# An output projection of eight K pairs as two products of 1024 columns, with the second half's keys rotated earlier, in a one-core encoder block

## The chip, the core and the metric

The kernel runs on one core of one Trainium2 chip. The core's engines work side by side, each with its own queue of instructions that it takes in order: TensorE (PE in the profile, with its weight loads as PEld), VectorE (DVE), ScalarE (ACT), GpSimd (POOL) and SyncE (SP), which here only issues transfers; 16 DMA engines carry data between HBM, in which inputs and weights lie, and the on-chip memory SBUF. TensorE writes into PSUM, a small memory of accumulators that VectorE and ScalarE read. A result passes from one engine to another by semaphores: an instruction that waits holds up everything behind it on its own engine.

The metric is the time of one execution on the device, in microseconds (us). Three executions of the kernel before took 1145.72, 1146.16 and 1146.77 us.

## The reference

One layer of an encoder over 256 tokens of width 2048, all in float32. Two groups of attention heads work side by side on the normalised input, and one matrix joins them:

```python
h = rms_norm(x, g_mix)
c_q, c_kv, k_rope, dq, dk, dv = jnp.split(h @ w_in, split_pts, axis=-1)
# latent attention: 8 heads with values of 128 -> out_mla (256 x 1024)
# differential attention: 4 heads, keys of 128, values of 256, rope on dq and dk
p1 = softmax(q1 @ k1.T * scale); p2 = softmax(q2 @ k2.T * scale)
o_diff = rms_norm((p1 - lam * p2) @ v, g_diff_sub, eps=1e-5) * (1 - lambda_init)
x = x + concatenate([out_mla, out_diff]) @ w_out          # 2048 x 2048
# cross attention: 4 heads of 128 into 256 tokens of mem
xq = rms_norm(x, g_xattn) @ w_xq
xk, xv = rms_norm(mem, g_mem) @ w_xk, rms_norm(mem, g_mem) @ w_xv
x = x + softmax(xq @ xk.T * scale) @ xv @ w_xo
# feed-forward with 5632 hidden columns
hf = rms_norm(x, g_ffn)
x = x + (silu(hf @ w_gate) * (hf @ w_up)) @ w_down
return rms_norm(x, g_final)
```

## The kernel before

**Matmuls.** Every float32 operand is split into a high part (`_h`), rounded to TensorE's float32r format, and a low part (`_l`), the remainder; a product is three matmuls, high by high, high by low and low by high (`mm`, L97 to L99). The split of weights costs ScalarE a cast (L105, `wh`) and VectorE a subtraction (L106, `wl`) for every 1024 columns of a 1 MB weight transfer (`wraw`, three buffers; `wh` and `wl` have four buffers each). The 256 tokens are two tiles of 128 (`tt` 0 and 1), the residual stream `x_res` (`xres0`, `xres1` in the profile) lies on chip as two tiles of 128 x 2048. Activations that go into a product lie transposed, four K blocks of 128 in a tile (`x0T`, `mixT`, `diffT`, `x1T`, `mT` ...).

**Two ways to multiply.** `project` makes 512 output columns from a list of weight pieces, with one accumulator for each token tile. `wide_project`, which before serves the feed-forward part alone, makes 1024 columns (two accumulators for each token tile) and goes over pairs of K blocks. A plain pair (`P`) is 2 x 2 x 2 products, 24 matmuls. A summed pair (`W`) takes a form of the product of two 2 x 2 block matrices with seven block products in place of eight, 21 matmuls. It needs sums of the activations' blocks (`summed_pair`: tiles `sums`, `forms`), sums of the weights' blocks (`tsum`), and four further accumulators (`q1`, `q5`, `q6`, `q7`) that are added at its end (`leave`), before the plain accumulators are (`join`). `_pairs` lays weights out in HBM for it, in the order `PLAIN` or `SUMS` of blocks.

**Stages.** The input projection and the latent attention come first and leave `mixT`, 8 K blocks. Differential attention comes in two halves of two heads each: `diff_project` and `diff_rope` make rotated queries and keys (`dT`), `values` the values (`val`), `diff_attend` scores (`psc`), softmax (`nm`, `e`, `rs`), the difference of two softmaxes (`e`), its transposes (`ppt`, `pT`), the product with the values (`pod`), the norm of each head (`ssd`, `rd`, on ScalarE, VectorE and GpSimd), the normalised head (`on`) and its transposes (`pdt`, `diffT`). The text order of the halves: queries, keys, values of the first half; queries of the second; attention of the first; keys and values of the second; attention of the second.

The output projection then comes in three pieces in columns of 512: `mixT` (8 K blocks), `diff0` (4), and, behind the keys of the memory (`mT` from a transfer with a gain, `w_xk`, `xkT`), `diff1` (4) inside `residual_T`. That function adds each column to `x_res`, transposes it with the gain of the next norm (`gT`, `x1T`) and sums its squares (`junk`). Cross attention and the feed-forward part follow.

**What sets the order.** The text names operations and dependences. A scheduler with a cost model of its own orders each engine's instructions when the kernel is built, and it interleaves stages: matmuls of a later stage stand between those of an earlier one where their operands and buffers allow it. The order on each engine is then fixed. Weight transfers keep the order of the text (`keep_in_program_order`), all on SP's queue. PSUM has eight banks: four accumulators (`acc_tile`) and four for everything else (`ps_tile`); `wide_project` swaps the two groups at its end.

Of the kernel before, what the change touches and what calls it, by code (L numbers as in the profile page):

```python
# [40 lines left out]
G_ORDER, U_ORDER = (0, 1, 2, 3, 4, 5, 6, 7), (0, 2, 1, 4, 3, 6, 5, 7)  # L41

# [36 lines left out]
def encoder_block(ctx: ExitStack, tc: tile.TileContext, a, out):  # L79
# [118 lines left out]
    def meansq(src, dst, cols, n):  # L198

        junk = sb.tile([P, 512], BF16, name="junk", tag="junk", bufs=1)  # L200
        nc.scalar.activation(junk[:, :cols], src, AF.Square, scale=n ** -0.5, accum_out=dst)

# [327 lines left out]
    def diff_attend(dq, dk, dv):  # L530
        mT = act_tile(name="diffT")
        ps_ = []
        for hh in range(2):
# [9 lines left out]
            ps_.append(e1)  # L543
        for hh in range(2):
# [19 lines left out]
            split_into(mT[:, 2 * hh:2 * hh + 2, :], pt.rearrange("p (e t) -> p e t", e=2))  # L564
        return mT
# [42 lines left out]
    def residual_T(src_accs, gain, name, raws=None):  # L608

        pieces = []  # L610
        ssq = small.tile([P, NT, 4], F32, name=name + "ss", tag=name + "ss", bufs=1)
        for oc in range(4):
            accs = src_accs(oc)
            t = act_tile(name=name)
            if raws is not None:
                raws.append(act.tile([P, 4, S], F32, name=name + "_f", tag="act"))
            for tt in range(NT):
                xs = x_res[tt][:, oc * 512:(oc + 1) * 512]
                nc.vector.tensor_tensor(out=xs, in0=xs, in1=accs[tt], op=ALU.add)
                transposed(t, xs, tt, 4, gain[:, 4 * oc:4 * oc + 4], raws and raws[oc])  # L620
                meansq(xs, ssq[:, tt, oc:oc + 1], 512, D)
            pieces.append(t)
        s1 = small.tile([P, NT], F32, name=name + "s1", tag=name + "s1", bufs=1)
        nc.vector.reduce_sum(out=s1, in_=ssq, axis=AX.X)
        r = rstd_of(s1, EPS, name + "r")
        return (lambda kt: pieces[kt // 4][:, kt % 4, :]), r
# [21 lines left out]
    x2raw = []  # L648
    x2T, rstdf = residual_T(
        lambda oc: project(lambda kt: xoT[:, kt, :], [a["w_xo"][oc, 0]]), g_f, "x2T", x2raw)  # L650
    soft_pool.close()
    attention.close()
    wsum = ctx.enter_context(tc.tile_pool(name="wsum", bufs=1))
    nat_pool[:] = wsum, 5


    def pair_raw(src):
        raw = wp.tile([P, 2048], F32, name="wraw", tag="wraw", bufs=3)
        raw = raw.rearrange("p (b c) -> p b c", b=4)
        tc.keep_in_program_order(nc.sync.dma_start(out=raw, in_=src))  # L660
        return raw

    def w_tile(n=2, pool=None):

# [4 lines left out]
    def split_blocks(src, pool=None):  # L669
        w = w_tile(src.shape[1], pool)  # L670
        split_into(w, src)
        return w

    class Pair:


        def __init__(self, plain=None, forms=None):
            self.plain, self.forms = plain, forms
# [351 lines left out]
```

## Time and profile before

| what | value |
|---|---|
| three executions | 1145.72, 1146.16, 1146.77 us |
| profiled execution | 1146.36 us |
| its span, from the first to the last instruction | 1144.6 us |
| mean granted clock of TensorE | 0.998 |
| TensorE busy | 1135.1 us (99%) |
| VectorE busy | 955.9 us (84%) |
| ScalarE busy | 636.2 us (56%) |
| GpSimd busy | 57.6 us (5%) |
| moved by DMA | 222.13 MB, 194 GB/s in the mean |
| transfers of w_out | 16 of 1 MB |

Busy times are sums over an engine's instructions in one profiled execution. Matmuls are pipelined, and the ends that the profile gives them are modelled, so that their pace is read from one start to the next. A name in the profile has a line of the kernel in front of it and shows a group of operations with the same output and input tiles. The chain of waits follows the work back from the last instruction, at each step to what released it. The granted clock is the share of full speed that the chip allowed TensorE.

In the trace the scores of the first half of differential attention lie around 250 us, the products of its probabilities and of the second half up to 290 us, the keys of the memory, the last piece of the output projection and the query of the cross attention from there to some 400 us; the feed-forward part fills the rest.

### The profile page before, as it was taken

To read this page: it belongs to the slowest core of one execution; us is meant where nothing else is said; L and a number is where in the kernel's file an instruction comes from. 1 tells how busy PE (TensorE), PEld (TensorE's weight loads), DVE (VectorE), ACT (ScalarE), POOL (GpSimd) and SP (SyncE) were. 2 spreads that over 40 slices of the span, in tenths; PEclk is the share of its full clock that TensorE was granted. 3 is DMA by queue.
4 is the path that set the end of the run, shared out by engine and by line. 5 is a ranking of instruction groups with operands and counts; after the bars stand their busy time and mean duration, and the time that the engine had idled before them with its cause. 6 is when DMAs were issued, how large, how long until landed. Compare 5 with 4: busy or idle time off the path is not lost.

```text
span 1144.6 us, 14297 instructions
## 1 busy us (share of the span) xinstructions
PE 1135.1 (99%) x5405; PEld 950.7 (83%) x5405; DVE 955.9 (84%) x1281; ACT 636.2 (56%) x897; POOL 57.6 (5%) x75
## 2 busy tenths in 40 slices
PE   9999999999999999999999999999999999999997
PEld 7888888888888888888888888888888888888886
DVE  6688766686868667989899998998999898998975
ACT  6755454454566455656465564665554564664642
POOL 4920000000000000000000000000000000000000
PEclk9999999999999999999999999999999999999999
DMA  9655335444854444455565556556555555565543
GB/s 358 221 194 187 143 113 182 154 178 155 318 194 179 148 166 169 180 192 208 197 212 194 182 213 221 184 187 218 184 190 215 201 204 191 195 242 202 195 171 129
DMA packets 34197, 222.13 MB, mean 194 GB/s; under 512 B 4176, under 2 KB 4944, under 8 KB 9808
## 3 DMA queue, kind: packets, MB, share of 16 engines
q1 hardware_dynamic: 32688, 216.73, 53.2%
q0 software_dynamic: 864, 3.15, 0.7%
q10 hardware_dynamic: 576, 1.34, 0.3%
q8 instruction: 42, 0.69, 0.2%
q14 instruction: 27, 0.22, 0.1%
HBM read 219.11 MB, written 2.10 MB: 193 GB/s over the span
## 4 chain that ended last, share of the span: by engine, by line
PE 98%; issue 0%; DMA 0%; DVE 0%; ACT 0%; DVEq 0%; POOLq 0%; POOL 0%; ACTq 0%
PE acc L97 27%; PE acc L98 26%; PE acc L99 26%; PE q L97 3%; PE q L99 3%; PE q L98 3%; PE pt L333 2%; PE ppt L480 1%; PE psc L99 1%; PE psc L98 1%; PE psc L97 1%; PE acckv L97 0%; PE acckv L98 0%; PE acckv L99 0%; PE pt L863 0%
## 5 line engine op out<-in xcount | busy, mean ns | idle before, releaser
L105 ACT CAST wh<-wraw 128x1024 fp32r<-128x1024 f32 (+2 forms) x400 | 392.5, 997 | 352.2 <-PE acc L99 305.5
L106 DVE TENSOR_TENSOR wl<-wraw,wh 128x1024 fp32r<-128x1024 f32 (+2 forms) x400 | 458.2, 1159 | 122.9 <-ACT wh L105 120.8
L98 PE MATMUL acc<-wl,x2n_h 128*128 128x512 f32 x320 | 124.5, 390 | 0.0
L99 PE MATMUL acc<-wh,x2n_l 128*128 128x512 f32 x320 | 123.9, 389 | 0.0
L106 DVE TENSOR_TENSOR wl<-tsum,wh 128x1024 fp32r<-128x1024 f32 x86 | 104.7, 1220 | 12.2 <-ACT wh L105 12.2
L105 ACT CAST wh<-tsum 128x1024 fp32r<-128x1024 f32 x86 | 90.2, 1050 | 42.7 <-DVE tsum L730 14.4
L97 PE MATMUL acc<-wh,x2n_h 128*128 128x512 f32 x320 | 109.7, 390 | 0.0
L98 PE MATMUL acc<-wl,x0T_h 128*128 128x512 f32 x224 | 88.3, 395 | 0.0
L99 PE MATMUL acc<-wh,x0T_l 128*128 128x512 f32 x224 | 88.2, 395 | 0.0
L97 PE MATMUL acc<-wh,x0T_h 128*128 128x512 f32 x224 | 87.3, 395 | 0.8 <-ACT x0T_h L108 0.8
L98 PE MATMUL acc<-wl,hT_h 128*128 128x512 f32 x188 | 73.3, 392 | 0.0
L99 PE MATMUL acc<-wh,hT_l 128*128 128x512 f32 x188 | 72.4, 389 | 0.0
L99 PEld LDWEIGHTS acc<-wh,x2n_l 128*128 128x128 f32 x320 | 60.1, 188 | 12.4
L98 PEld LDWEIGHTS acc<-wl,x2n_h 128*128 128x128 f32 x320 | 60.1, 188 | 12.3
L97 PEld LDWEIGHTS acc<-wh,x2n_h 128*128 128x128 f32 x320 | 59.9, 188 | 12.3
L98 PE MATMUL q<-wl,forms_h 128*128 128x512 f32 x172 | 66.9, 389 | 0.0
L99 PE MATMUL q<-wh,forms_l 128*128 128x512 f32 x172 | 66.7, 389 | 0.0
L97 PE MATMUL acc<-wh,hT_h 128*128 128x512 f32 x188 | 64.5, 391 | 0.0
L97 PE MATMUL q<-wh,forms_h 128*128 128x512 f32 x172 | 59.9, 389 | 0.0
L98 PE MATMUL acc<-wl,forms_h 128*128 128x512 f32 x149 | 57.8, 389 | 0.0
L99 PE MATMUL acc<-wh,forms_l 128*128 128x512 f32 x149 | 57.8, 389 | 0.0
L97 PE MATMUL acc<-wh,forms_h 128*128 128x512 f32 x149 | 57.0, 389 | 0.0
(382 smaller groups left out, 2258.0 us busy)
## 6 DMA issues: line engine op xcount, KB each, us to landing
wraw<-in_w_gate SPq DMA_DIRECT2D x44, 1024.0 KB, 4.8
wraw<-in_w_up SPq DMA_DIRECT2D x44, 1024.0 KB, 4.8
wraw<-in_w_dn SPq DMA_DIRECT2D x41, 1024.0 KB, 4.8
wraw<-in_w_in SPq DMA_DIRECT2D x24, 1024.0 KB, 4.8
wraw<-in_w_out SPq DMA_DIRECT2D x16, 1024.0 KB, 4.8
wraw<-in_w_in_lat SPq DMA_DIRECT2D x7, 832.0 KB, 7.8
wraw<-in_w_xk SPq DMA_DIRECT2D x4, 1024.0 KB, 6.0
wraw<-in_w_xq SPq DMA_DIRECT2D x4, 1024.0 KB, 4.8
```

Source lines behind the costliest of these rows:

```text
L97: nc.tensor.matmul(o, l.h, r.h, start=start, stop=False)
L98: nc.tensor.matmul(o, l.h, r.l, start=False, stop=False)
L99: nc.tensor.matmul(o, l.l, r.h, start=False, stop=stop)
L105: last_cast[0] = nc.scalar.copy(out=dst.h, in_=src).ins
L106: last_split[0] = nc.vector.tensor_tensor(out=dst.l, in0=src, in1=dst.h.bitcast(F32), op=ALU.subtract).ins
L333: nc.tensor.transpose(out=pt[:, j * P:(j + 1) * P], in_=src[:, j * P:(j + 1) * P], identity=ident)
L480: nc.tensor.transpose(out=pt[:, kt * S + tt * P:kt * S + (tt + 1) * P], in_=p[:, tt, kt * P:(kt + 1) * P], identity=ident)
```

## The change

The output projection is now made by `wide_add`, as two products of 1024 columns over all eight K pairs: four from `mixT` (pairs 0 to 3), two from the first half of differential attention (pairs 4 and 5), two from the second (6 and 7). `OUT_KINDS` makes pairs 4 and 5 summed ones, `OUT_ORDERS` gives the order of the pairs in each product. `w_out` is laid out by `_pairs` to match. For that, `wide_project`, `wide_add`, `summed_pair` and what they call stand earlier in the text, and their tiles of sums come from the pool of activations until the feed-forward part has its own; `tsum` is two tiles of half the size.

`diff_attend` becomes two functions, `diff_probs` (scores to probabilities) and `diff_heads` (values to transposed heads, or the forms of a summed pair). In the new text order the keys of the second half are rotated ahead of the first half's heads, and its scores come ahead of its values. Each product is followed by the transposes of its two columns (`column_T`), and the keys of the memory come behind both products. `residual_T` is gone; its second use, after the cross attention, is written out with `column_T`.

```diff
+OUT_KINDS, OUT_ORDERS = "PPPPWWPP", ((0, 1, 2, 3, 4, 6, 5, 7), (0, 1, 2, 4, 3, 6, 5, 7))
...
+    def sums_tile(name, dtype=F32):
+        pool, tag = (act, "act") if sum_pool[0] is None else (sum_pool[0], name)
+        return pool.tile([P, 2, 512], dtype, name=name, tag=tag, bufs=24 if sum_pool[0] is None else 1)
...
     def wide_project(pairs, src, order, kinds, leave, join, closed=(0, 1)):
...
-            t = wsum.tile([P, 4, 512], F32, name="tsum", tag="tsum", bufs=1)
+            t01, t23 = [sums_tile(name) for name in ("tsum", "tsum2")]
...
-    def diff_attend(dq, dk, dv):
-        mT = act_tile(name="diffT")
+    def diff_probs(dq, dk):
         ps_ = []
...
             ps_.append(e1)
+        return ps_
+
+    def diff_heads(ps_, dv, kinds):
+        mT = act_tile(name="diffT") if "P" in kinds else None
+        pairs = []
         for hh in range(2):
             pT = prob_T(ps_[hh])
...
-            split_into(mT[:, 2 * hh:2 * hh + 2, :], pt.rearrange("p (e t) -> p e t", e=2))
-        return mT
+            pt = pt.rearrange("p (e t) -> p e t", e=2)
+            if kinds[hh] == "W":
+                pairs.append(summed_pair(pt[:, :, :P], pt[:, :, P:], True))
+                continue
+            m = mT[:, 2 * hh:2 * hh + 2, :]
+            split_into(m, pt)
+            pairs.append(Pair(m))
+        return pairs
...
-    def add_mix(piece_of, xT, n):
-        for oc in range(4):
-            add_out(project(xT, [piece_of(oc, i) for i in range(n)]), oc)
...
-    diff0 = diff_attend(dq0, dk0, dv0)
+    probs = diff_probs(dq0, dk0)
     dk1 = diff_rope(diff_project(1, 1))
+    diff0 = diff_heads(probs, dv0, OUT_KINDS[4:6])
+    probs = diff_probs(dq1, dk1)
     dv1 = values(diff_project(1, 2), rstd1)
-    diff1 = diff_attend(dq1, dk1, dv1)
-    add_mix(lambda oc, i: a["w_out"][0, oc, i], lambda kt: mixT[kt // 4][:, kt % 4, :], 2)
-    add_mix(lambda oc, i: a["w_out"][1, oc, i], lambda kt: diff0[:, kt, :], 1)
+    diff1 = diff_heads(probs, dv1, OUT_KINDS[6:])
+
+    def column_T(t, oc, tt, gain, ssq, raw=None):
+        xs = x_res[tt][:, oc * 512:(oc + 1) * 512]
+        transposed(t, xs, tt, 4, gain[:, 4 * oc:4 * oc + 4], raw)
+        meansq(xs, ssq[:, tt, oc:oc + 1], 512, D)
...
+    mix = [Pair(t[:, k:k + 2, :]) for t in mixT for k in (0, 2)] + diff0 + diff1
+    x1p = []
+    x1ss = small.tile([P, NT, 4], F32, name="x1ss", tag="x1ss", bufs=1)
+    for h in range(2):
+        wide_add(mix, a["w_out"][h], OUT_ORDERS[h], OUT_KINDS, 2 * h)
+        for oc in (2 * h, 2 * h + 1):
+            x1p.append(act_tile(name="x1T"))
+            for tt in range(NT):
+                column_T(x1p[oc], oc, tt, g_x, x1ss)
+    rstdx = rstd_of_sums(x1ss, "x1T")
...
     mT = Transposed(a["memT"], g_m, "mT")
     acc = project(mT, [a["w_xk"][i] for i in range(4)], before=mT.load)
...
-    def residual_T(src_accs, gain, name, raws=None):
...
-    x1T, rstdx = residual_T(
-        lambda oc: project(lambda kt: diff1[:, kt, :], [a["w_out"][1, oc, 1]]), g_x, "x1T")
...
-        "w_out": np.stack([_pieces(w_out[:1024]), _pieces(w_out[1024:])]),
+        "w_out": _pairs(i["w_out"][0], OUT_KINDS),
```

The order of instructions on two engines at three places follows; rows are line, operation, output and inputs, shape, and a number behind a name tells tiles of one name apart.

TensorE before, behind the scores of the second half (`psc_2469` is the last of four). `acc_2643` is the accumulator of a column of the `mixT` piece; 41 such matmuls stand here before the first transpose of the probabilities:

```order
L97 MATMUL psc_2469<-dT_h_2239,dT_h_1913 128x256
L98 MATMUL psc_2469<-dT_l_2240,dT_h_1913 128x256
L99 MATMUL psc_2469<-dT_h_2239,dT_l_1914 128x256
L97 MATMUL acc_2643<-wh_2647,mixT_h_1093 128x512
L98 MATMUL acc_2643<-wl_2648,mixT_h_1093 128x512
L99 MATMUL acc_2643<-wh_2647,mixT_l_1094 128x512
L97 MATMUL acc_2644<-wh_2647,mixT_h_1093 128x512
```

The same place now, where `ppt_2515` transposes the probabilities `e_2303` of the half's first head and `acc_2598` is an accumulator of the first product for the second token tile:

```order
L99 MATMUL psc_2347<-dT_h_2157,dT_h_1913 128x256
L100 MATMUL psc_2347<-dT_l_2158,dT_h_1913 128x256
L101 MATMUL psc_2347<-dT_h_2157,dT_l_1914 128x256
L631 MATMUL ppt_2515<-ident_101,e_2303 128x128 x4
L99 MATMUL acc_2598<-wh_2602,mixT_h_1093 128x512
L100 MATMUL acc_2598<-wl_2603,mixT_h_1093 128x512
```

The transposes now follow the scores without anything between them.

TensorE now, at the end of the first half's heads (`pod_2249` is the product of its second head, `on_2270` the normalised head, `pdt_2273` its transposes, `psc_2293` the first scores of the second half):

```order
L99 MATMUL pod_2249<-val_h_1769,pT_h_2245 128x256
L100 MATMUL pod_2249<-val_l_1770,pT_h_2245 128x256
L101 MATMUL pod_2249<-val_h_1769,pT_l_2246 128x256
L719 MATMUL pdt_2273<-ident_101,on_2270 128x128
L99 MATMUL psc_2293<-dT_h_2157,dT_h_1913 128x256
L100 MATMUL psc_2293<-dT_l_2158,dT_h_1913 128x256
```

Before, this head's transposes stood behind matmuls of the projection of the second half's values:

```order
L98 MATMUL acc_2270<-wl_2380,x0T_h_363 128x512
L99 MATMUL acc_2270<-wh_2379,x0T_l_364 128x512
L562 MATMUL pdt_2094<-ident_101,on_2091 128x128 x4
L97 MATMUL acc_2571<-wh_2575,mixT_h_1093 128x512
L98 MATMUL acc_2571<-wl_2576,mixT_h_1093 128x512
```

VectorE now, right behind the four joins that end the second product: the transposed columns (`gT`, `x1T_l`), and the first piece of the memory (`mT_l`) with the first weights of its keys:

```order
L488 TENSOR_TENSOR gT_3281<-pt_3276,gains_98 128x512
L488 TENSOR_TENSOR gT_3292<-pt_3287,gains_98 128x512
L488 TENSOR_TENSOR gT_3305<-pt_3300,gains_98 128x512
L488 TENSOR_TENSOR gT_3316<-pt_3311,gains_98 128x512
L108 TENSOR_TENSOR x1T_l_3275<-gT_3281,x1T_h_3274 128x4x128
L756 TENSOR_REDUCE x1Ts1_3322<-x1ss_2595 128x2
L108 TENSOR_TENSOR x1T_l_3275<-gT_3292,x1T_h_3274 128x4x128
L108 TENSOR_TENSOR x1T_l_3299<-gT_3305,x1T_h_3298 128x4x128
L196 TENSOR_SCALAR x1Tr_3324<-x1Ts1_3322 128x2
L108 TENSOR_TENSOR x1T_l_3299<-gT_3316,x1T_h_3298 128x4x128
L111 SCALAR_TENSOR_TENSOR mT_l_3330<-xraw_3331,gains_98,mT_h_3329 128x256 x4
L108 TENSOR_TENSOR wl_3344<-wraw_3341,wh_3343 128x1024
```

Before, the pieces of the memory stood between splits of weights and the adds of `w_out`'s columns (L570):

```order
L570 TENSOR_TENSOR xres0_108<-xres0_108,acc_2787 128x512
L570 TENSOR_TENSOR xres1_109<-xres1_109,acc_2788 128x512
L106 TENSOR_TENSOR wl_2906<-wraw_2899,wh_2905 128x1024
L109 SCALAR_TENSOR_TENSOR mT_l_3014<-xraw_3015,gains_98,mT_h_3013 128x256 x4
L106 TENSOR_TENSOR wl_2940<-wraw_2937,wh_2939 128x1024
L106 TENSOR_TENSOR diffT_l_2414<-pdt_2564,diffT_h_2413 128x512
L570 TENSOR_TENSOR xres0_108<-xres0_108,acc_2859 128x512
```

The columns of `x1T` have moved ahead of `mT_l`.

More of the change, by code (lines that the diff above doesn't have):

```diff
@@ new lines, in wide_result, with leave, join @@
+    def wide_result(pairs, src, order, kinds):
+        res = []
+        def leave(Q):
+            res[:] = [act.tile([P, 2, 512], F32, name=f"res{tt}", tag="act") for tt in range(NT)]
+            q1, x, v, y = res[0][:, 0, :], res[0][:, 1, :], res[1][:, 0, :], res[1][:, 1, :]
+            nc.scalar.copy(out=q1, in_=Q[1])
+            nc.vector.tensor_tensor(out=v, in0=Q[6], in1=q1, op=ALU.subtract)
+            nc.vector.tensor_tensor(out=x, in0=Q[5], in1=v, op=ALU.add)
+            nc.vector.tensor_tensor(out=v, in0=v, in1=Q[7], op=ALU.subtract)
+            nc.vector.tensor_tensor(out=y, in0=Q[5], in1=v, op=ALU.add)
+        def join(tt, oc, acc):
+            r = res[tt][:, oc, :]
+            nc.vector.tensor_tensor(out=r, in0=acc, in1=r, op=ALU.subtract if (tt, oc) == (1, 0) else ALU.add)
+        wide_project(pairs, src, order, kinds, leave, join)
+        return res
```

248 lines of the change are left out of this document (117 added, 131 removed).

## The prediction

> **What bounds the kernel now.** I read the page first, then the waits of TensorE, then busy time by stretch. From the page:
>
> ```profile
> span 1144.6 us, 14297 instructions
> PE 1135.1 (99%) x5405; PEld 950.7 (83%) x5405; DVE 955.9 (84%) x1281; ACT 636.2 (56%) x897; POOL 57.6 (5%) x75
> PE 98%; issue 0%; DMA 0%; DVE 0%; ACT 0%; DVEq 0%; POOLq 0%; POOL 0%; ACTq 0%
> ```
>
> TensorE is busy 99% of the span, and the chain of waits lies on it for 98%. The view of what TensorE waited for (engine, tile and line; what it waited for; us in total, times, longest) has nothing longer than 1.2 us:
>
> ```profile
> PE wps L215 <- DVE warm L209: 1.2, 1, 1.2
> PE acc L97 <- ACT x0T_h L108: 0.8, 1, 0.8
> PE po L97 <- ACT val_h L108: 0.2, 1, 0.2
> ```
>
> The stretches that the change rewrites (columns: stretch, length, then busy us and count of PE, PEld, DVE, ACT, POOL, granted clock, DMA share, GB/s) show no gap on TensorE and the full clock:
>
> ```profile
> 210.00:290.00 80.00, 80.00 (x404) 67.69 (x403) 55.08 (x88) 38.94 (x67) 5.15 (x8) 1.00 0.50 178
> 290.00:410.00 120.00, 119.80 (x578) 99.88 (x577) 89.65 (x128) 71.87 (x123) 1.41 (x2) 1.00 0.57 205
> ```
>
> So the time is the number of matmuls times their pace, and there is no idle TensorE time that an edit could recover. VectorE has work for 70 to 75% of these stretches: every wait on it is hidden by matmuls that TensorE has queued in the meantime. The question is what an edit saves in matmuls, and what hidden wait it uncovers.
>
> The pace, from start to start, in rows of the timeline (start, us to the modelled end, instruction):
>
> ```profile
> 444.94 0.39 PE L98 MATMUL acc<-wl,x2T_h 128*128 128x512 f32 x1
> 445.16 0.39 PE L99 MATMUL acc<-wh,x2T_l 128*128 128x512 f32 x1
> ...
> 251.13 0.28 PE L98 MATMUL psc<-dT_l,dT_h 128*128 128x256 f32 x1
> 251.25 0.28 PE L99 MATMUL psc<-dT_h,dT_l 128*128 128x256 f32 x1
> ...
> 337.18 1.03 PE L333 MATMUL pt<-ident,xk 128*128 128x128 f32 x8
> 337.97 0.48 PE L97 MATMUL acc<-wh,diffT_h 128*128 128x512 f32 x1
> ```
>
> A 512-column matmul takes 0.22 to 0.23 us (I use 0.227, over several rows), a 256-column one 0.12, a transpose about 0.1 (eight in 337.97 − 337.18 = 0.79).
>
> **The change part by part.** *Summed pairs.* A plain pair of K blocks is 24 matmuls, a summed one 21. Two pairs of eight are summed, in two products: 12 fewer, 12 × 0.227 = **−2.7 us**. All other matmuls and transposes stay; the same 16 MB of w_out comes by the same 1 MB transfers on SP's queue, so I cost the loads at nothing: in 210 to 410 us the DMA engines are busy 50 to 57%, which is the cover.
>
> *The first wait: normalising the second head of the first half (A).* In the new order on TensorE the products of the second head (pod) are followed directly by their transposes (pdt). Before, matmuls of the projection of the values stood between. The chain between them, as it runs before:
>
> ```profile
> 284.15 0.28 PE L99 MATMUL pod<-val_h,pT_l 128*128 128x256 f32 x1
> 284.46 0.38 ACT L201 ACTIVATE junk<-pod 128x256 bf16<-128x256 f32 x1 [1.70 <-PE pod L99]
> 285.48 0.17 DVE L194 TENSOR_SCALAR rd<-ssd 128x2 f32<-128x2 f32 x1 [1.46 <-ACT junk L201]
> 285.79 0.69 POOL L195 TENSOR_TENSOR rd<-rd,mhalf 128x2 f32<-128x2 f32 x1 [15.03 <-DVE rd L194]
> 286.52 0.88 DVE L557 SCALAR_TENSOR_TENSOR on<-pod,rd,gdb 128x256 f32<-128x256 f32 x2 [0.87 <-POOL rd L195]
> ```
>
> TensorE is free at 284.15 + 0.12 = 284.27; the first of the two `on` ends at 286.52 + 0.44 = 286.96 and, by my estimate, reaches TensorE about 0.1 later: **+2.8** (2.6 if nothing lies between, 3.3 if both `on` are awaited). The scores of the second half, queued behind pdt, wait with it; they could have been the cover.
>
> *The second wait: the softmax of the second half's first head (B).* Behind pdt stand the 24 score matmuls and 3 transposes, 24 × 0.12 + 3 × 0.1 = 3.2 us, then ppt, which wants the probabilities. Before, 41 matmuls of mixT stood at this place. Rows of the same chain in the first half:
>
> ```profile
> 251.40 1.28 DVE L464 TENSOR_REDUCE nm<-psc 128x2 f32<-128x512 f32 x2
> 252.60 0.16 DVE L465 TENSOR_SCALAR nm<-nm 128x2 f32<-128x2 f32 x1
> 252.85 0.48 ACT L469 ACTIVATE e<-psc,nm 128x256 f32<-128x256 f32 x1 [3.10 <-DVE nm L465]
> 254.10 0.62 DVE L539 TENSOR_SCALAR e<-e,rs 128x256 f32<-128x256 f32 x2
> 255.28 0.88 DVE L541 SCALAR_TENSOR_TENSOR e<-e,nr 128x256 f32<-128x256 f32 x2
> ...
> L691 DVE TENSOR_TENSOR sums<-a,pt x8: 277/280/281, 576.5 to 1065.0; 128x128 f32<-128x128 f32 x8
> ```
>
> The first psc is done 6 × 0.12 + 0.28 = 1.0 us after the scores start; two reductions (1.28) and one small operation (0.16) end at 2.4. From there VectorE's own queue up to the finished probabilities holds two more reductions (1.28), four differences of the new forms (4 × 0.28, the last row), the scaling (0.62), the combination (0.88) and seven small ones of about 0.16: 5.0 us, hence 7.4, and the wait is 7.4 − 3.2 = 4.2. Without the queue the chain is 2.4 + (256.16 − 252.85) = 5.7, a wait of 2.5. Some of the queue lies beside ScalarE's exponentials; I take **+4.0** (2.5 to 4.9), near the queue's sum, since only one queue serves both.
>
> *The third wait: the banks of the values (C).* After ppt TensorE goes on with acc for the second 128 tokens, in PSUM banks that the projection of the values held. They come free with val_l:
>
> ```profile
> 246.02 1.40 DVE L109 SCALAR_TENSOR_TENSOR val_l<-acc,rstd,val_h 128x512 fp32r<-128x512 f32 x2
> ```
>
> In the new order of VectorE there stand between the probabilities and val_l two forms (0.42 and 0.68, estimated as the halves and the whole of a 512-column subtraction) and a scaling (0.62); with val_l (0.70) 2.4 us, less the four transposes of ppt (0.4): **+2.0** (1.2 to 2.5). Fillers are used up: the accumulators that have banks have consumed the pairs of weights that fit the four buffers.
>
> *Summed pairs on VectorE (W).* Groups of the page (busy us, mean ns of one):
>
> ```profile
> L106 DVE TENSOR_TENSOR wl<-wraw,wh 128x1024 fp32r<-128x1024 f32 x340 | 411.0, 1223 | 106.9 <-ACT wh L105 105.2
> L730 DVE TENSOR_TENSOR tsum<-wraw 128x1024 f32<-128x1024 f32 x43 | 52.4, 1218 | 0.5 <-DMA wraw<-in_w_up 0.3
> L734 DVE TENSOR_TENSOR tsum<-tsum,wraw 128x512 f32<-128x512 f32 x43 | 29.4, 684 | 0.1
> ```
>
> A plain pair costs VectorE 2 × 1.22 = 2.4 against 24 × 0.227 = 5.4 on TensorE. A summed one costs three splits of 1.22, one of half that width (0.69), one sum of 1.22 and two of 0.68: 6.9 against 4.8. The product as a whole: 6 × 2.4 + 2 × 6.9 + twelve adds of 0.64 to 0.68 (8.0) + columns (four gT, four x1T_l of 0.68, 5.5) = 41.7, against 6 × 5.4 + 2 × 4.8 = 42.0. So VectorE just keeps up over a product, but loses 2.1 per summed pair where it happens. The plain pairs ahead leave it 3 us each, and the buffers of split weights hold two pairs of that lead. I take **+1.0**, near the low end, since the loss shows only once that lead of some 6 us is used up; ends are 0 and 4 × 2.1 = 8.4.
>
> *The fourth wait: the keys of the memory (D).* Before, they stood ahead of the last piece on diff1, whose 84 matmuls were queued between the keys and the cross attention. Now they stand behind the last column. The rows:
>
> ```profile
> 288.44 1.28 DVE L570 TENSOR_TENSOR xres<-xres,acc 128x512 f32<-128x512 f32 x2
> L337 DVE TENSOR_TENSOR gT<-pt,gains 128x512 f32<-128x512 f32 x10 | 6.6, 686 | 1.2 <-PE pt L333 1.2
> L106 DVE TENSOR_TENSOR x1T_l<-gT,x1T_h 128x512 fp32r<-128x512 f32 x8 | 5.3, 684 | 0.0
> 290.21 1.71 ACT L108 ACTIVATE mT_h<-xraw,gains 128x256 fp32r<-128x256 f32 x4 [0.58 <-DMA xraw<-in_memT]
> 290.80 1.67 DVE L109 SCALAR_TENSOR_TENSOR mT_l<-xraw,gains,mT_h 128x256 fp32r<-128x256 f32 x4
> ```
>
> Counted from TensorE's last matmul of the product: the accumulators end 0.45 apart, so that VectorE's fourth join ends 1.4 later (four of 0.64, the first 1.2 before the end); then come four gT (2.7), four x1T_l (2.7), four mT_l (1.7) and the split of w_xk's first pair (1.2): 9.7. TensorE has in this time 16 transposes (16 × 0.1 = 1.6, with their own waits some 2.1) and two matmuls that want only the high halves (0.45): **+7.1**. The order of VectorE is fixed, so that mT_l cannot go ahead of x1T_l even where its transfer has landed. Lower end 6.1 (ScalarE's casts overlap and a join less); upper end 12, if the adds of the summed pairs are still ahead of the joins.
>
> *The clock.* At the program's start, the chain of waits (start, us, what) shows matmuls at half pace for a while, and at the end the granted clock falls when TensorE has nothing to do:
>
> ```profile
> 5.54 1.22 PE acc L97 x2
> ...
> 7.29 0.85 PE acc L98 x2
> ...
> 9.99 0.23 PE acc L97
> ```
>
> ```profile
> 1136.95 0.28 PE L99 MATMUL acc<-w_h,forms_l 128*128 128x256 f32 x1
> ...
> 1135.00:1140.00 5.00, 2.23 (x19) 2.03 (x17) 3.78 (x12) 1.68 (x2) 0.56 (x1) 0.96 0.55 210
> 1140.00:1144.60 4.60, 0.00 (x0) 0.00 (x0) 0.23 (x1) 0.00 (x0) 0.00 (x0) 0.50 0.60 228
> ```
>
> Half pace is 0.85 / 2 = 0.427 us a matmul, from 5.54 to 9.99: 4.45 us, of which 1 − 0.227 / 0.427 = 0.47 is lost, 2.1 us a restart. The fall: 5 × 0.96 is 0.2 us short of full, half of which is lost rate, so the clock halves about 0.4 before 1140, some 2.4 us after the last matmul. Pauses of 2.8, 4.0 and 7.1 can reach that. I take two restarts, one for the cluster A to C and one for D: **+4.2**; ends are 0 (transposes count as work and keep the clock) and 8.4 (four restarts).
>
> The Trainium skill ("TensorE: Matmul & The Clock Gate", Part 1, "What's actually happening") says that the clock is halved after at least one idle window of about 3.4 us and freed after one busy window, and that the windows run free. By that rule A and C could not halve it, B only by luck, and D likely; the sum would be one restart, 2.1 less. The fall after some 2.4 us in this trace says that a pause shorter than that figure can suffice, so the trace keeps two.
>
> Sum: −2.7 + 2.8 + 4.0 + 2.0 + 1.0 + 7.1 + 4.2 = **+18.4**. The profiled execution took 1146.36 us (span 1144.6), 0.2 above the median of 1146.16, so the median becomes **1164.6**.
>
> **The rivals.** *The waits come without a loss of clock.* Transposes and score matmuls between the pauses keep the clock up. For it: at the end of the program nothing at all ran for 2.4 us before the fall. Against it: B and D alone hold longer pauses. 18.4 − 4.2 = 14.2, with shorter waits (the lower ends of B, C and D, 3.3 less) 11: 1157 to 1160.5.
>
> *VectorE becomes the bound in the summed pairs.* All four lose 2.1, and the leaving adds push D on to 12: +8.4 − 1.0 and up to +4.9, 1169 to 1177. For it: 6.9 against 4.8. Against it: the lead of the plain pairs ahead.
>
> *Half the waits are filled*, because VectorE runs ahead of the queue as I counted it and weights arrive sooner: 1148.5 to 1156. Against it: the order on both engines is fixed and was counted by rows.
>
> *The other side: no wait is uncovered.* TensorE's queue is so far behind VectorE that the chains end in time, and only the 12 matmuls count: 1146.2 − 2.7 = 1143.5. Decisive is whether TensorE reaches pdt, ppt and the keys of the memory later than VectorE delivers; that needs some 3 us of other matmuls at each place, and the new order has none at the first and the last. For it: no wait over 1.2 us exists before.
>
> **How the numbers follow.** Waits with a loss of clock, 1160.5 to 1169: 0.55. Waits without it: 0.18. VectorE as the bound: 0.12. Half the waits filled: 0.06. Gain alone, or nearly (1143 to 1148.5): 0.09. The range 1156 to 1171 leaves out the gain, half of the filled waits and half of the bound VectorE, about 0.2. A measurement of this kernel can tell 0.2% from no change, that is 1143.9 to 1148.5: faster 0.07, within 0.2% 0.03, slower 0.90.
>
> **What would show it.** In the changed profile the waits of TensorE should list pdt behind `on` with about 2.8 us, ppt behind e with about 4, acc behind val_l with about 2, and acc of the memory's keys behind wl with about 7; the stretch of the heads and the stretch behind the second product should show a clock under 1.00. Matmuls of 512 columns should number 12 fewer. The forecast is wrong if these waits are absent or under a microsecond, if summed pairs show waits for tsum's splits of more than 1 us each, or if the clock stays at 1.00 throughout; in the last case the time is about 4 us lower.

## The result, and the profile after

The changed kernel takes **1167.67 us** in the median of six executions (1166.24 to 1169.03), the kernel before 1146.09 (1145.72 to 1146.77). The ratio is 1.0187, with a 95% interval of 1.0174 to 1.0200: 21.6 us slower, where 1164.6 us (18.4 slower) was forecast with a range of 1156 to 1171.

The page of the changed kernel, the lines that answer to those of before:

```profile
span 1166.7 us, 14318 instructions
PE 1141.7 (98%) x5393; PEld 952.2 (82%) x5393; DVE 972.0 (83%) x1313; ACT 644.0 (55%) x913; POOL 59.8 (5%) x75
PE 91%; DVE 4%; DMA 2%; ACT 1%; issue 1%; POOL 0%; DVEq 0%; POOLq 0%; ACTq 0%
```

TensorE has its 12 matmuls fewer (5393 for 5405), yet is busy 6.6 us longer, because some of them run at half pace, and the chain of waits lies on it for 91% in place of 98%. What TensorE waited for now:

```profile
PE acc L99 <- ACT wh L107: 6.8, 3, 5.3
PE pdt L719 <- DVE on L714: 2.6, 1, 2.6
PE ppt L631 <- DVE e L692: 2.0, 1, 2.0
...
PE acc L99 <- DVE val_l L111: 1.2, 1, 1.2
```

The four waits of the prediction's last part are there: pdt behind `on`, ppt behind `e`, acc behind `val_l`, and the keys of the memory, whose pause the view puts down to the high halves of the weights (`wh`, longest 5.3 us). Busy time by stretch in the changed kernel, the heads and then the end of the second product:

```profile
242.00:265.00 23.00, 16.69 (x78) 13.99 (x77) 13.57 (x37) 10.99 (x33) 0.69 (x1) 0.78 0.00 1
340.00:360.00 20.00, 14.32 (x62) 11.08 (x62) 19.57 (x35) 15.48 (x31) 3.40 (x5) 0.83 0.58 213
```

These two stretches hold most of the loss: up to the first product that reads `x2T_l`, which opens the feed-forward part, the profiled executions are 17.1 us apart (436.3 us before, 453.4 now), at the end 22.1. In the heads VectorE is not the bound: it works 13.6 of 23 us, and no weight arrives (DMA share 0.00), since SyncE's next transfer of `w_out` waits, 27.0 us at the longest, for a split that frees a buffer. At the end of the second product VectorE works 19.6 of 20 us, so that it may be the bound there; run 1 tests that. The chain of waits at that place (start, us, what) shows the fourth wait step by step:

```profile
343.49 1.28 DVE xres L348 x2
344.77 2.39 DVE gT L488 x4
347.16 0.60 DVE x1T_l L108
...
349.70 0.39 DVE mT_l L111
...
351.29 1.15 DVE wl L108
```

This is the queue that the prediction added up: joins, columns, the low half of the memory's first piece, the split of its weights. From TensorE's last matmul of the product at 343.22, with its 0.23, to the end of the split at 352.44 it takes 9.0 us, where 9.7 was forecast.

A third place was not in the forecast. From 735 to 1060 us, in the feed-forward part, TensorE waited for nothing before. In the changed kernel it waits there as follows, and the same stretch, shown for before and then for the changed kernel, holds 19 matmuls fewer:

```profile
PE acc L100 <- DVE wl L108: 1.5, 3, 0.6
PE acc L99 <- ACT wh L107: 1.5, 2, 0.8
```

```profile
735.00:1060.00 325.00, 325.00 (x1458) 269.43 (x1457) 302.26 (x356) 182.06 (x214) 1.10 (x2) 1.00 0.57 204
```

```profile
735.00:1060.00 325.00, 321.93 (x1439) 264.82 (x1437) 296.25 (x356) 182.40 (x218) 1.10 (x2) 1.00 0.57 199
```

### The profile page after: what moved, and what is told of

It reads as the page before. It is cut to its first block, busy times and chain, and to the rows that moved or that the text cites. A ratio compares the mean times of both kernels' runs of the same rounds, so it can differ in the third digit from the quotient of the medians.

```text
span 1166.7 us, 14318 instructions
## 1 busy us (share of the span) xinstructions
PE 1141.7 (98%) x5393; PEld 952.2 (82%) x5393; DVE 972.0 (83%) x1313; ACT 644.0 (55%) x913; POOL 59.8 (5%) x75
## 4 chain that ended last, share of the span: by engine, by line
PE 91%; DVE 4%; DMA 2%; ACT 1%; issue 1%; POOL 0%; DVEq 0%; POOLq 0%; ACTq 0%
PE acc L99 24%; PE acc L100 24%; PE acc L101 24%; PE q L99 3%; PE q L101 3%; PE q L100 3%; DVE wl L108 2%; PE pt L484 2%; DMA wraw<-in_w_down 1%; DMA wraw<-in_w_up 1%; PE psc L99 1%; PE psc L100 1%; PE psc L101 1%; PE ppt L631 1%; ACT wh L107 1%
## 5 line engine op out<-in xcount | busy, mean ns | idle before, releaser
L107 ACT CAST wh<-tsum 128x1024 fp32r<-128x1024 f32 x94 | 97.8, 1050 | 44.4 <-DVE tsum L290 19.1
L108 DVE TENSOR_TENSOR wl<-tsum,wh 128x1024 fp32r<-128x1024 f32 x94 | 113.6, 1218 | 7.6 <-ACT wh L107 7.0
L100 PE MATMUL q<-wl,forms_h 128*128 128x512 f32 x188 | 73.2, 389 | 0.0
L101 PE MATMUL q<-wh,forms_l 128*128 128x512 f32 x188 | 73.0, 389 | 0.0
L99 PE MATMUL q<-wh,forms_h 128*128 128x512 f32 x188 | 66.4, 390 | 0.0
L285 DVE TENSOR_TENSOR tsum<-wraw 128x1024 f32<-128x1024 f32 x47 | 57.2, 1218 | 7.7 <-DMA wraw<-in_w_up 4.7
L100 PE MATMUL acc<-wl,forms_h 128*128 128x512 f32 x161 | 62.5, 391 | 1.2 <-DVE wl L108 1.2
L99 PE MATMUL acc<-wh,forms_h 128*128 128x512 f32 x161 | 61.7, 391 | 1.6 <-ACT wh L107 1.5
```

Of the source, the lines that this page charges most:

```text
L99: nc.tensor.matmul(o, l.h, r.h, start=start, stop=False)
L100: nc.tensor.matmul(o, l.h, r.l, start=False, stop=False)
L101: nc.tensor.matmul(o, l.l, r.h, start=False, stop=stop)
L107: last_cast[0] = nc.scalar.copy(out=dst.h, in_=src).ins
L108: last_split[0] = nc.vector.tensor_tensor(out=dst.l, in0=src, in1=dst.h.bitcast(F32), op=ALU.subtract).ins
L285: nc.vector.tensor_tensor(out=t01, in0=raw[:, 1:3, :], in1=raw[:, 0:1, :].to_broadcast([P, 2, 512]), op=ALU.add)
```

## The experiments

Runs 1 to 5 and 8 edit the changed kernel; runs 6, 7 and 9 to 12 start from run 5, which carries the two edits that had removed waits. Each was compared with the kernel before on the same chip, which took 1145.5 to 1146.0 us.

**1. The keys of the memory ahead of the last columns.**

```diff
     for h in range(2):
         wide_add(mix, a["w_out"][h], OUT_ORDERS[h], OUT_KINDS, 2 * h)
+        if h == 1:
+            mT = Transposed(a["memT"], g_m, "mT")
+            acc = project(mT, [a["w_xk"][i] for i in range(4)], before=mT.load)
+            ...                                  # to xkT, as it was
         for oc in (2 * h, 2 * h + 1):
```

> The changed kernel with one move: the keys of the memory stand between the second product and the transposes of its columns, instead of behind them. Theory 1 (the loss sits in the pauses of TensorE, and what the clock loses behind each): the pause behind the second product (5.5 us, with 0.3 before it and 0.6 behind it) and the half-pace matmuls after it (about 1.7) go, 8.1 in all: 1159.6 us (1158 to 1161). Theory 2 (VectorE has more work than it can do there, and TensorE waits for it in one place or another): the wait moves into the keys or the columns, 1165 to 1169.

Measured: 1160.35 us (1158.79 to 1160.42), 7.3 less. In 340 to 360 us TensorE is busy throughout at the full clock, although VectorE has no free moment there:

```profile
340.00:360.00 20.00, 20.00 (x90) 16.57 (x89) 19.99 (x31) 15.98 (x31) 0.00 (x0) 1.00 0.77 277
```

The loss of the fourth wait, with the half pace behind it, came from the place of the keys. That VectorE simply had too much to do at this place falls.

**2. Attention of the halves in the old order of the text.**

```diff
-    probs = diff_probs(dq0, dk0)
+    diff0 = diff_heads(diff_probs(dq0, dk0), dv0, OUT_KINDS[4:6])
     dk1 = diff_rope(diff_project(1, 1))
-    diff0 = diff_heads(probs, dv0, OUT_KINDS[4:6])
-    probs = diff_probs(dq1, dk1)
     dv1 = values(diff_project(1, 2), rstd1)
-    diff1 = diff_heads(probs, dv1, OUT_KINDS[6:])
+    diff1 = diff_heads(diff_probs(dq1, dk1), dv1, OUT_KINDS[6:])
```

> The changed kernel with one move: attention of the first half as a whole before the second half's keys and values, then attention of the second half, as the text of the kernel before had it; the product stays as changed. Theory 1: the pauses at pdt, ppt and acc (2.8, 3.0 with its small ones, 1.6) and about 4 of half pace go, 11.5 in all: 1156.2 us (1154.5 to 1158). Theory 2 (the forms of the summed pairs load VectorE there, so that other waits of like length appear, whatever the order): 1163 to 1168.

Measured: 1170.68 us (1169.28 to 1171.93), no gain at all: 3.0 more. The old waits are gone, and others stand in 200 to 300 us:

```profile
PE acc L99 <- DVE dn L476: 3.6, 1, 3.6
PE acc L99 <- ACT wh L107: 2.6, 2, 2.4
```

So theory 2 was right here in that other waits appear, although the time lies above its 1163 to 1168. That the second half's keys and scores come sooner in the text is not needed for pauses of this size. What the first row says was found with run 7.

**3. Both moves.**

> Both moves together. Theory 1: the two gains add, 1167.7 - 8.1 - 11.5 = 1148.1 us (1146.5 to 1150), with 12 matmuls fewer and about 4.5 us of waits left in the feed-forward part against the kernel before. Theory 2: 1160 or more. If the feed-forward waits come and go with the order that the scheduler happens to find, the time may be up to 4.5 lower or higher than theory 1 says.

Measured: 1161.80 us (1160.20 to 1162.17). Against run 2 the keys again bring 8.9, against run 1 the old order of the heads costs 1.5. To within 1.6 us the two stretches are independent of each other.

**4. One tile of sums in the feed-forward part.**

```diff
-            t01, t23 = [sums_tile(name) for name in ("tsum", "tsum2")]
+            if sum_pool[0] is None:
+                t01, t23 = [sums_tile(name) for name in ("tsum", "tsum2")]
+            else:
+                t = wsum.tile([P, 4, 512], F32, name="tsum", tag="tsum", bufs=1)
+                t01, t23 = t[:, 0:2, :], t[:, 2:4, :]
```

> The changed kernel with the sums of weights in the feed-forward part as one tile of four blocks again, as in the kernel before; the rest as changed. Theory A (the two half tiles of sums cause the five new waits of TensorE in the feed-forward part, some 4.6 us): 1163.1 us (1162 to 1164.5), without those waits. Theory B (the scheduler orders the feed-forward part otherwise because what comes before it has another length): waits of 2 us or more stay there, 1165.5 to 1169.

Measured: 1162.73 us (1161.49 to 1163.89), 4.9 less, and TensorE again waits for nothing from 735 to 1060 us:

```profile
735.00:1060.00 325.00, 325.00 (x1457) 269.47 (x1457) 301.69 (x360) 183.29 (x218) 1.10 (x2) 1.00 0.58 206
```

Theory B wanted waits of 2 us or more to stay, so it falls: the split of one tile into two made this loss. From the first product that reads `x2T_l` to the end, the profiled executions take 708.3 us before, 713.3 in the changed kernel and 708.5 here. The operations and their sizes are the same; how two tiles in place of one lead to these waits was not followed further.

**5. Both edits together.**

> Both edits that removed waits so far, on the changed kernel: the keys of the memory ahead of the last columns, and one tile of sums in the feed-forward part. If the losses are separate pauses, the gains add: 1167.7 - 7.3 - 4.9 = 1155.5 us (1154 to 1157), and what is left against the kernel before is the stretch of the heads alone, 2.7 less and some 12 more. If they are one shortage of VectorE that moves about, 1158 or more.

Measured: 1154.13 us (1153.21 to 1155.84). The gains add (7.3 + 4.9 = 12.2, measured 13.5). What is left against before is 8.1 us, and of the waits that the kernel before has not, all over 0.2 us stand in the heads: pdt 2.6, ppt 2.2 and `val_l` 1.2.

**6. The same, all pairs plain.**

```diff
-OUT_KINDS, OUT_ORDERS = "PPPPWWPP", ...
+OUT_KINDS, OUT_ORDERS = "PPPPPPPP", ...
```

> As the run with both edits, but all eight pairs plain: 12 matmuls more (+2.7 us), no forms and no sums. In the order that results, 24 matmuls of mixT stand between the second head's products and its transposes, and 38 around the end of the second half's scores. Theory 1 (the pauses of the heads come from the summed pairs of this half, which take VectorE's time and so empty TensorE's queue there): no pause over 1 us in the heads, 1155.5 + 2.7 - 11.9 = 1146.3 us (1145 to 1148.5), the time of the kernel before. Theory 2 (they come from scores and heads being moved, whatever the pairs are): the pauses stay, 1157 to 1159.

Measured: 1147.43 us (1146.66 to 1147.79, ratio to before 1.0013, interval 1.0004 to 1.0023). With 12 matmuls more, 6.7 us are won, and of TensorE's waits in 200 to 300 us these are left:

```profile
PE pdt L723 <- DVE on L718: 0.6, 1, 0.6
PE pod L99 <- ACT pT_h L107: 0.3, 1, 0.3
```

The order of VectorE shows how. In the plain kernel the values of the second half (`val_l_2484`) stand ahead of the second head's norm and of the softmax:

```
L111 SCALAR_TENSOR_TENSOR val_l_2484<-acc_2345,rstd1_510,val_h_2483 128x512
L111 SCALAR_TENSOR_TENSOR val_l_2484<-acc_2346,rstd1_510,val_h_2483 128x512
L196 TENSOR_SCALAR rd_2256<-ssd_2251 128x2
L718 SCALAR_TENSOR_TENSOR on_2259<-pod_2238,rd_2256,gdb_1430 128x256 x2
```

In the trace of the plain kernel they start at 238.43 us, `on` at 245.12. In the changed kernel they stand behind both, among the forms, as its chain of waits shows (they are its step ahead of the first product for the second token tile, which waits for them):

```profile
252.63 0.78 DVE e L692 x2
253.42 0.34 DVE forms_l L108
253.75 0.52 DVE e L690 x2
254.27 0.60 DVE forms_l L108
254.87 0.67 DVE val_l L111
```

`val_l` frees the two PSUM banks in which the products for the second token tile accumulate. Where it is early, 24 matmuls of mixT for that tile stand between pod and pdt, and more around the scores; where it is late, there is nothing to stand there. By these rows the prediction's first and third wait had one cause, and the second is there for want of the same filler. This is read from the orders and not shown by an experiment: no run moves `val_l` forward alone, with the summed pairs kept.

**7. The product over mixT in columns of 512 again.**

```diff
+    for oc in range(4):
+        add_out(project(lambda kt: mixT[kt // 4][:, kt % 4, :], [a["w_out_m"][oc, i] for i in range(2)]), oc)
-    mix = [Pair(t[:, k:k + 2, :]) for t in mixT for k in (0, 2)] + diff0 + diff1
+    mix = diff0 + diff1
```

The heads follow the old text order of run 2, and `OUT_KINDS` for these four pairs is "WWPP".

> As the run with both edits, but the product over mixT is made in columns of 512 again, with two accumulators at a time, attention of the halves follows the old text order, and only the four pairs of differential attention (two of them summed) go through the products of 1024 columns. Theory of the banks (a product of 1024 columns holds four of PSUM's accumulators, so that TensorE's filling work waits for banks that projections hold): no pause over 1 us in the heads. But each product of 1024 columns now has 2 plain and 2 summed pairs for the same adds and columns: VectorE 2 x 2.4 + 2 x 6.9 + 13.5 = 32 us against some 22 on TensorE, so that up to 10 us are lost in each, less what the keys of the memory cover: 1148 to 1158. If pauses in the heads stay, the banks were not their cause: 1156 to 1168.

Measured: 1160.61 us (1159.93 to 1161.53). The pause for `dn` is there as in run 2 with 3.6 us, so that four accumulators in place of two for the product over mixT are not its cause. VectorE's rows tell more. Here the rotation (`ropetmp`, `dn`), which frees the banks of the keys' projection, begins at 238.36. Two splits of weights stand ahead of it, the second of which waits 1.13 us for its high half, and the first difference of a form:

```profile
233.88 0.88 DVE L718 SCALAR_TENSOR_TENSOR on<-pod,rd,gdb 128x256 f32<-128x256 f32 x2 [0.81 <-POOL rd L197]
234.67 1.22 DVE L108 TENSOR_TENSOR wl<-wraw,wh 128x1024 fp32r<-128x1024 f32 x1
237.02 1.23 DVE L108 TENSOR_TENSOR wl<-wraw,wh 128x1024 fp32r<-128x1024 f32 x1 [1.13 <-ACT wh L107]
238.16 0.28 DVE L246 TENSOR_TENSOR sums<-a,pdt 128x128 f32<-128x128 f32 x1
238.36 0.42 DVE L478 TENSOR_TENSOR ropetmp<-acc,sind 128x256 f32<-128x256 f32 x1
```

In the kernel before it followed `on` at once:

```profile
233.00 0.88 DVE L557 SCALAR_TENSOR_TENSOR on<-pod,rd,gdb 128x256 f32<-128x256 f32 x2 [0.81 <-POOL rd L195]
233.80 0.41 DVE L323 TENSOR_TENSOR ropetmp<-acc,sind 128x256 f32<-128x256 f32 x1
```

In both text orders, then, a VectorE operation that frees banks stands later once heads are summed. Here the splits hold it back more than the form does (0.28 us), and that the summed heads brought the splits to this place is read from the comparison with before, not tested. The rest of the time goes in the products and the keys: in 300 to 360 us TensorE waits 5.2 us for the splits of the summed pairs (4.7 and 0.5 by its waits) and 2.9 for those of the memory's keys. The first part is the rival of a VectorE that becomes the bound: it lies in the second product, where one plain pair runs ahead of two summed ones and VectorE has the first product's columns to do.

**8. Spare matmuls in the fourth wait.**

```diff
+    with tc.issue_after(last_T[0]):               # the last transpose of the columns
+        spare = ps_tile("spare")
+        for _ in range(44):
+            nc.tensor.matmul(spare[:, :256], x1p[0].h[:, 0, :P], x1p[0].h[:, 1, :], start=True, stop=True)
```

> The changed kernel with 44 matmuls of 256 columns that nobody reads, put on TensorE between the last transposes of the columns and the keys of the memory (5.2 us at full pace, in a pause of 5.5). Theory of the clock (the pause costs its own length and, behind it, half pace until the clock is full again): the half pace behind the pause goes, 1.4 us less, 1166.3 us, and the granted clock stays at 1.00 there. Rival (the slow matmuls behind the pause are slow because their operands come late): no gain, 1167.7, or the length of what the spare matmuls overrun, up to 1169.

Measured: 1167.26 us (1166.84 to 1167.34). The granted clock (the third number from the right) of the changed kernel and then with the spare matmuls:

```profile
346.00:349.00 3.00, 0.00 (x0) 0.00 (x0) 3.00 (x7) 3.00 (x8) 0.00 (x0) 0.84 0.00 0
349.00:352.00 3.00, 0.98 (x2) 0.50 (x2) 3.00 (x8) 3.00 (x6) 2.81 (x4) 0.50 0.08 16
352.00:355.00 3.00, 2.76 (x7) 2.04 (x7) 3.00 (x6) 3.00 (x6) 0.59 (x2) 0.52 0.97 268
```

```profile
346.00:349.00 3.00, 3.00 (x27) 3.00 (x26) 3.00 (x8) 3.00 (x9) 0.47 (x1) 1.00 0.00 0
349.00:352.00 3.00, 2.28 (x15) 1.64 (x14) 3.00 (x7) 3.00 (x6) 2.95 (x5) 1.00 0.34 78
352.00:355.00 3.00, 3.00 (x14) 2.46 (x15) 3.00 (x6) 3.00 (x6) 0.00 (x0) 1.00 0.90 313
```

So much is shown: with work in the pause the clock stays full. The time hardly follows (0.4 less in the median, within what the two ranges leave open, where 1.4 was expected). In the traces TensorE is 1.1 us further on behind the pause: the second pair of matmuls by the high halves of the keys' weights starts 10.7 us behind the last twelve transposes of the columns, 11.8 in the changed kernel. But in 735 to 1060 us it then waits 2.5 us for `wl`, 1.5 in the changed kernel. Why it waits longer there was not followed.

**9 and 10. One summed head.** `OUT_KINDS` is "PPPPWPPP" (the first head of the first half), then "PPPPPWPP" (the second).

> As the run with both edits, but only the first head of the first half is summed (pair 4), the second is plain: 6 matmuls fewer than all plain. In the order that results, the pause between the second head's products and its transposes has no filling work, but 24 matmuls of mixT stand between the scores and ppt. If the forms of the second head, which stand on VectorE among the second half's softmax and ahead of its values, make the second and third pause, then the first pause (2.8) stays with about 1 of half pace, the others go: 1147.4 - 1.4 + 3.8 = 1149.8 us (1148 to 1151.5). If summing any pair of this half does it: 1154 to 1156.

> The counterpart: only the second head of the first half is summed (pair 5). If the forms of the second head make the pauses, all three stay with their half pace, 11.9, and 6 matmuls are saved against all plain: 1147.4 - 1.4 + 11.9 = 1157.9, less what a lighter product gives back, so 1154 to 1158 us. If the load of two summed pairs on VectorE is what counts, about half of it: 1149 to 1153.

Measured: 1159.39 us (1158.19 to 1159.85) with the first head, 1155.57 (1155.13 to 1157.22) with the second. TensorE's longest waits from 200 to 300 us, first and second:

```profile
PE acc L99 <- ACT wh L107: 2.9, 2, 2.4
PE pdt L723 <- DVE on L718: 2.6, 1, 2.6
PE acc L99 <- DVE val_l L111: 1.7, 1, 1.7
```

```profile
PE pdt L723 <- DVE on L718: 2.6, 1, 2.6
PE ppt L635 <- DVE e L696: 2.1, 1, 2.1
PE acc L99 <- DVE val_l L111: 1.2, 1, 1.2
```

One summed pair costs no less than two: against the kernel before on the same chip, run 9 is 13.9 us slower and run 10 10.1, where run 5 with both is 8.1 slower. Run 10 came as expected for the second head's forms; run 9 missed by 9.6 us, since with the first head summed a like loss stands in other places. In both, `val_l` stands behind the first reductions of the softmax on VectorE (at 250.20 and 255.06 us). The loss does not grow with the load. That it hangs on the order on VectorE fits these rows, and no run shows it alone.

**11 and 12. Summed pairs of mixT.** Pair 2 ("PPWPPPPP"), then pairs 2 and 3 ("PPWWPPPP"); `heads_out` of the latent attention makes the forms, and the heads of differential attention stay plain.

> As the run with all pairs plain, but one pair of mixT summed (pair 2, its forms made in the latent attention), last but one in the first product: 6 matmuls fewer. If a summed pair costs nothing where its forms are not in the way of softmax and values and where plain pairs ahead give VectorE a lead: 1147.4 - 1.4 = 1146.0 us (1145 to 1147.5), the time of the kernel before. If VectorE pays for it wherever it stands: 1148 to 1152.

> Two pairs of mixT summed (pairs 2 and 3), differential attention plain: the 12 matmuls fewer of the change, without its place. If place alone decides: 1147.4 - 2.7 = 1144.7 us (1143.5 to 1146.5), 0.1% under the kernel before. In the first product the two summed pairs follow one another, where VectorE needs 6.9 for each against 4.8 on TensorE, so 2 to 4 may be lost there: 1146 to 1149. If VectorE pays wherever they stand: 1150 or more.

Measured: 1169.50 us (1168.13 to 1170.27) and 1173.12 (1172.21 to 1174.60), far off. In run 11 the heads of differential attention are as quiet as in run 6 (no wait over 0.6 us in 200 to 300 us); in run 12 pdt waits 2.6 us for `on`. The latent attention is quiet in neither. Its stretch with all pairs plain and with one summed:

```profile
95.00:135.00 40.00, 40.00 (x219) 34.52 (x218) 32.29 (x61) 19.35 (x36) 0.00 (x0) 1.00 0.44 157
```

```profile
95.00:135.00 40.00, 28.38 (x180) 25.19 (x179) 26.86 (x69) 19.74 (x52) 0.00 (x0) 0.85 0.00 1
```

No weight comes in for 40 us, and the projections that fill this stretch are missing. By SyncE's own waits the next transfer of weights in run 11 stood 47.0 us behind VectorE's `neg_lam`, in run 12 53.6 us behind a `forms_l`. VectorE's rows in run 11 show what lies ahead of that:

```profile
87.03 1.21 DVE L108 TENSOR_TENSOR wl<-wraw,wh 128x1024 fp32r<-128x1024 f32 x1
...
127.23 0.41 DVE L478 TENSOR_TENSOR ropetmp<-acc,sind 128x256 f32<-128x256 f32 x1
...
133.18 2.35 DVE L108 TENSOR_TENSOR wl<-wraw,wh 128x1024 fp32r<-128x1024 f32 x2
135.46 0.15 DVE L682 SCALAR_TENSOR_TENSOR neg_lam<-lexp 128x1 f32<-128x1 f32 x1
```

From 88 to 133 us VectorE splits no weights, so that none of the three buffers of a transfer comes free; `neg_lam` is only the small operation that follows the splits. The rotation of the first half's queries stands at 127.23, in run 6 at 98.05, and the projection after it begins at 129.65, in run 6 at 99.50. With forms made in the latent attention, the order has moved this whole stretch of work back by some 30 us; what in the edit moved it was not tested.

This stop covers what the times of the two runs could say of a summed pair where VectorE has time, but the traces of the products say a part. In the first product, with six plain pairs ahead of the summed one in run 11 and five ahead of two in run 12, TensorE waits for none of their splits. In the second product of run 11, where the summed pair is the third and VectorE still has the first product's columns to do, it waits 3.0 us (2.0 at the same place in run 12), against 1.4 us that the pair saves in both products:

```profile
PE q L99 <- ACT wh L107: 3.0, 2, 2.7
```

No version that beats the kernel before was found.

## Why the prediction was right

- **The bound and the sign.** TensorE without idle time before, hence nothing to win but 12 matmuls, and every hidden wait that loses its cover a loss: that held. All four named waits appeared. The rows near 250 and 285 us of the kernel before, from which A and B were costed, are those of the second half of differential attention and not of the first, whose scores start at 194 us; both halves run the same operations, so that the sums stand.
- **A**, forecast +2.8: TensorE stood from 242.49 to 245.40, 2.9 from start to start and 2.8 without the last matmul's own 0.12.
- **B**, +4.0: about 3.4 in pieces, the longest 2.2. The scores that cover it ran in part at half pace, 0.21 us each for 0.12, since A had already taken the clock down. They did not only cover the softmax: the chain of waits runs over these scores, twelve of them at 0.21 us, until 249.75, where the third reduction (`nm`) can start, and over VectorE from there. From the first score at 245.48 to ppt at 253.17 it took 7.7 us, where 7.4 was added up.
- **C**, +2.0: 1.6.
- **W**, +1.0: about 0.8 of short waits between 278 and 281 us. The lead of the plain pairs carried it, as taken: in the second product three of them run ahead of the first summed pair, and TensorE waits for none of its splits. With two ahead it waits 3.0 us there (run 11), with one 5.2 (run 7).
- **D**, +7.1: 6.4 in the trace (5.5, and 0.3 and 0.6 around it). The queue was the one added up; VectorE's operations overlap a little (four `gT` of 0.68 take 2.47), so that it took 9.0 in place of 9.7.
- **The clock**, +4.2 as two restarts: 4.5 in all by the matmuls that took 0.43 us in place of 0.227 (0.21 in place of 0.12 for the scores). Of these, 3.1 lie in the heads, some 1.3 at the scores behind A and 1.8 at the products behind C, and 1.4 behind D. So the clock fell three times and not twice, and the size came out near. That the time would be lower by as much with a full clock is not shown: run 8 kept it full at D, won 1.1 there and lost most of it again later. The rule of the Trainium skill ("TensorE: Matmul & The Clock Gate", Part 1, "What's actually happening"), by which D and only by luck B would have cost it, does not fit this trace: a pause of 2.8 us was enough.
- **What was missing**: the feed-forward part. The prediction costed only the products of w_out and took the rest as it stood. `sums_tile`, which it did not speak of, cost 4.9 us by run 4. Without this loss (1162.73 us in run 4) the forecast would have been 1.9 above the time; with it the sum falls 3.1 short. Both times lie in the range, which so held a term that it was not made for. Together the measured terms are −2.7 + 2.8 + 3.4 + 1.6 + 0.8 + 6.4 + 4.5 + 4.9 = 21.7, where the spans differ by 22.1.
- **Where the explanation was too narrow.** The sum took the order on the two engines as given, and that served it well. But it read A, B and C as prices of the moved scores. Runs 2 and 6 say otherwise: with the scores where they are and plain pairs the pauses go, with the scores moved back and summed pairs others come. They are the price of the summed heads: by runs 5 and 6 these cost 9.4 us (6.7 of them net) for 2.7 saved.

## What to carry to other kernels

In a program whose TensorE is busy throughout, ask of each added VectorE operation not how long it is, but which operation behind it frees a buffer or bank that TensorE's filling work needs: here, by the orders, 24 matmuls of cover hung on one `val_l`. Where a compiler's scheduler sets the order, read the new order on every engine over the whole program, places far from the edit too; a tile split in two cost as much here as a real wait. And a saving in matmuls is worth their pace only as long as no pause opens that takes the clock down; in this kernel pauses of 2.2 and 2.8 us did.

## What the runs showed of the hardware

The clock of TensorE fell in pauses of 2.2 us and more, and also though short work stood between. In the changed kernel, in stretches of 3 us behind the last matmul of the first half's heads at 242.49 (the granted clock is the third number from the right):

```profile
242.00:245.00 3.00, 0.77 (x7) 0.56 (x5) 0.31 (x2) 0.95 (x4) 0.69 (x1) 1.00 0.00 0
245.00:248.00 3.00, 2.60 (x13) 2.61 (x14) 1.43 (x3) 0.00 (x0) 0.00 (x0) 0.61 0.00 0
248.00:251.00 3.00, 2.58 (x17) 2.29 (x15) 2.37 (x10) 2.09 (x9) 0.00 (x0) 0.82 0.00 0
251.00:254.00 3.00, 0.96 (x6) 0.68 (x4) 3.00 (x13) 2.99 (x11) 0.00 (x0) 0.75 0.00 0
```

With the clock either full or half, as rows of 1.00 and 0.50 have it, a row of 0.61 has half clock for 2.3 of its 3 us. So the clock was down from 245.7 on, some 3 us after the last matmul of the heads, with a transpose and the first score between. It came back at 249.1 within the scores. The row of 0.75 has half clock for its last 1.5 us: the clock fell again at 252.5, 1.5 us after the last score started its 0.12 us at 250.85, inside a pause that ended with ppt at 253.17. In the fourth wait the row from 346 us with 0.84 puts the fall at 348.0, some 2.4 us after the last transpose of the columns. Run 8 shows that spare matmuls in such a pause keep the clock full.
